# adaLN products of a two-layer mixer: split weights and VectorE sums replaced by unsplit float32 matmuls in four 128x32 tiles

## The chip, the cores and the metric

The kernel runs on one core of one Trainium2 chip. The metric is the device time of one execution in microseconds; the time before is the median of 3 runs. Profiles and traces show one execution each.

## What is computed

Two trunk layers work on 1024 latent tokens of 1024 channels and 256 context tokens. Cut to what matters here:

```python
sc, scc = silu(c), silu(c_ctx)
for l in range(2):
    shift, scale, gate = split(sc @ w_ada[l] + b_ada[l], 3)           # w_ada[l]: 1024 x 3072
    shift_c, scale_c, gate_c = split(scc @ w_ada[l] + b_ada[l], 3)
    hc = rms_norm(h_ctx, norm_g[l]) * (1 + scale_c) + shift_c
    hx = rms_norm(x, norm_g[l]) * (1 + scale) + shift
    px = hx @ w_in[l]                    # queries, keys, values, GLU pair, Fourier input, three gates
    y = concat(attention * silu(g_att), conv_branch * silu(g_conv), fourier * silu(g_four)) @ w_out[l]
    if l == 0:
        h_ctx = h_ctx + gate_c * y_ctx   # the same mixer on the context tokens
    x = x + gate * y
return rms_norm(x, final_g)
```

All is float32. The adaLN products are two vectors (latent and context stream) times a 1024 x 3072 matrix, once for each layer.

## The kernel before, in words

Large float32 products are made as three float32r matmuls: each operand is split into a high part (a rounded copy, mostly ScalarE, `split`, line 373) and the rest (a subtraction, line 374, on GpSimd or VectorE), and `mm3` (lines 160 to 162) adds high x high, high x low and low x high in PSUM.

The order on each engine is set by a scheduler from priorities and its own estimates of time. Code inside `later()` gets a low priority and fills gaps; `later(0)` lets a block take turns with what follows. Loads are issued by SP, in one queue, in the order that the scheduler chose. Every engine works its own list in order. TensorE's accumulators are eight PSUM banks; `mmx` hands out two `pt` banks and one `mm` bank in turn.

The program runs so. The first layer's scale and shift come as columns for two blocks of 128 channels at a time (`ada_cols`, four times, u = 0 to 3). They are needed by `norm_transpose`, which transposes normed tiles on TensorE, applies scale and shift on ScalarE (line 361) and splits the result on VectorE (lines 363, 365). Three groups of tokens (512, 512, 256) pass, and a first pair of tiles of `w_in`, the Fourier input, is multiplied at once (`Pair`, p0, p1, p2). Then, for each layer: the second layer's scale and shift (`ada1`, in layer 0 alone), the GLU input of the convolution (`glu(0)`, `glu(1)`), the Fourier branch, the convolution's 31 taps on VectorE (`conv_taps`, lines 499 and 506, inside `later()`), the Fourier gate (`gate_mul`, lines 464 and 465), the sums for the residual gate (`gate_sums`, inside `later()`), keys, queries with rotary, values, attention mixed with more projections (the convolution's norm `conv_norm`, line 525, among them), then `gate_reduce` and the output projection.

The adaLN products are made in three ways:

- First layer, scale and shift (`ada_cols`): weights of 512 rows x 256 columns are loaded (16 loads of 512 KB), split on ScalarE and VectorE or GpSimd, and multiplied by `s4`, four columns (high and low of both streams), line 254. The four rows that result are transposed back to columns (line 263) and combined on VectorE (lines 265 to 277).
- Second layer, scale and shift (`ada_sums`, `ada_cols1`): weights of 128 rows x 1024 columns are loaded, and VectorE sums weight times scalar over eight loads for each stream (lines 286 and 288); TensorE then sums over partitions with a one-column matmul for each block of 128 channels (line 297).
- Gates of both layers (`gate_sums`, `gate_reduce`): the same VectorE sums, the bias added on one partition (line 313), and a sum over the partitions on every partition with a full matmul of ones (line 321).

Of the kernel before, what the change touches and what calls it, by code (L numbers as in the profile page):

```python
# [41 lines left out]
def f32(t):  # L42
    return t.bitcast(F32)


class Bufs:
    """Buffers of 1024 words (latent tokens) and of 256 words (context tokens), handed out by hand."""
# [18 lines left out]
class Buf:  # L66
# [19 lines left out]
    def again(self, what, dtype, ctx=True):  # L86
        """the same memory under another name; without ctx the short part is put back"""
        if not ctx and self.ic is not None:
            self.owner.free[256].append(self.ic)
            self.ic = None  # L90
        parts = [None if i is None else self.owner.named(what, i, words, dtype)
                 for i, words in ((self.il, 1024), (self.ic, 256))]
        self.il = self.ic = None
        return Buf(self.owner, *parts)
# [8 lines left out]
class Four:  # L103
    """four short buffers in the place of a long one"""
# [14 lines left out]
def tile_backbone(ctx: ExitStack, tc: tile.TileContext, a, out):  # L119
# [26 lines left out]
    def mmx():  # L146
        """an accumulator where no attention is about"""
        turn[0] += 1
        return mm() if turn[0] % 3 == 0 else pt()

    @contextmanager
    def later(offset=100000):
        """instructions that only fill gaps, or without an offset take turns with those that follow"""
# [10 lines left out]
    def rstd_of(ss, n, scale):  # L164
        """(ss * scale + EPS) ** -0.5 for columns [128, n] by Newton's iteration. A step without its factor of
        -1/2 multiplies by -2, -8 and -512; a power of two in v and the sign of the first guess make up for it."""
# [17 lines left out]
    ident = const.tile([P, P], F32, name="ident")  # L184
    prm = const.tile([P, 96], F32, name="prm")
    s2 = const.tile([P, 2, NK], F32, name="s2")
    s4 = const.tile([P, NK, 4], F32R, name="s4")
# [7 lines left out]
    def load_params():  # L195
# [6 lines left out]
        sv = s2.rearrange("p s k -> p (s k)")  # L202
        th16 = sm.tile([P, 16], F32, name="rv")
        S.activation(th16, prm[:, 0:16], AF.Tanh, scale=0.5)
        V.scalar_tensor_tensor(out=sv, in0=th16, scalar=1.0, in1=prm[:, 0:16], op0=ALU.add, op1=ALU.mult)
        V.tensor_scalar(out=sv, in0=sv, scalar1=0.5, scalar2=None, op0=ALU.mult)
        # columns c high, c low, ctx high, ctx low
        s4v = s4.rearrange("p k (s x) -> p s k x", x=2)
        V.tensor_copy(out=s4v[:, :, :, 0], in_=s2)
        V.tensor_tensor(out=s4v[:, :, :, 1], in0=s2, in1=f32(s4v[:, :, :, 0]), op=ALU.subtract)  # L210
# [15 lines left out]
    # scale (1) and shift (0) of two blocks of channels: [section, stream, block]  # L226
# [8 lines left out]
    def ada_cols(u, his):  # L235
        """the first layer's scale and shift of both streams as columns, for the channels of blocks 2u, 2u + 1"""
        l = 0
        oo = av(), mm()
        los, chain = [], Chain()
        for sec in (1, 0):  # L240
            o = oo[sec][0:4, 0:256]
            for h in range(2):
                j = (1 - sec) * 2 + h
                raw, lo = chain.next("wada")
                los.append(lo)
                wh, wl = his[(4 * u + j) % len(his)].lat, los[j].lat
                c0 = sec * D + u * 256
                nc.sync.dma_start(out=raw.lat.rearrange("p (r c) -> p r c", r=4),
                                  in_=a["w_ada"][l, h * 512:(h + 1) * 512, c0:c0 + 256]
                                  .rearrange("(r p) c -> p r c", p=P))  # L250
                split(wh, wl, raw.lat, (G if (4 * u + j) % 3 == 2 else V))
                for r in range(4):
                    for i, w in enumerate((wh, wl)):
                        T.matmul(o, lhsT=s4[:, h * 4 + r, :], rhs=w[:, r * 256:(r + 1) * 256],
                                 start=(h == 0 and r == 0 and i == 0), stop=(h == 1 and r == 3 and i == 1))
        for z in los + [chain]:
            z.put()
        t = t512()[0:4]
        S.activation(t[:, 256:512], oo[1][0:4, 0:256], AF.Copy)
        V.tensor_copy(out=t[:, 0:256], in_=oo[0][0:4, 0:256])  # L260
        b = oo[1][:, 256:272]
        for j in range(4):
            T.transpose(out=b[:, 4 * j:4 * j + 4], in_=t[:, j * P:(j + 1) * P], identity=ident[0:4, 0:4])
        q = sm.tile([P, 16], F32, name="nwt")
        V.tensor_copy(out=q, in_=b)
        qv = q.rearrange("p (e k s x) -> p e s k x", e=2, k=2, s=2)
        c = adac[u]
        for sec in range(2):
            V.tensor_tensor(out=c[:, sec], in0=qv[:, sec, :, :, 0], in1=qv[:, sec, :, :, 1], op=ALU.add)
        b0 = cols["b_ada"] + 24 * l + 2 * u  # L270
        g0 = cols["norm_g"] + 8 * l + 2 * u
        for st in range(2):
            x = c[:, 1, st]
            V.scalar_tensor_tensor(out=x, in0=x, scalar=1.0, in1=prm[:, b0 + 8:b0 + 10], op0=ALU.add, op1=ALU.add)
            V.tensor_tensor(out=x, in0=x, in1=prm[:, g0:g0 + 2], op=ALU.mult)
            x = c[:, 0, st]
            V.tensor_tensor(out=x, in0=x, in1=prm[:, b0:b0 + 2], op=ALU.add)

    def ada_sums(l, sec, streams, acc, wbufs):
        """a section on the vector engine: partial sums over the partitions' rows"""  # L280
        for k in range(NK):
            w = wbufs[k % len(wbufs)]
            nc.sync.dma_start(out=w, in_=a["w_ada"][l, k * P:(k + 1) * P, sec * D:(sec + 1) * D])
            for st, z in zip(streams, acc):
                if k == 0:
                    V.tensor_scalar(out=z, in0=w, scalar1=s2[:, st, 0:1], scalar2=None, op0=ALU.mult)
                else:
                    V.scalar_tensor_tensor(out=z, in0=w, scalar=s2[:, st, k:k + 1], in1=z,
                                           op0=ALU.mult, op1=ALU.add)

    def ada_cols1(sec, acc):
        """the second layer's scale or shift as columns"""
        b = mmx()[:, 0:2 * NK]
        for st in range(2):
            for k in range(NK):
                j = st * NK + k
                T.matmul(b[:, j:j + 1], lhsT=acc[st][:, k * P:(k + 1) * P], rhs=onesm[:, 0:1], start=True, stop=True)
        b0 = cols["b_ada"] + 24 + 8 * sec
        g0 = cols["norm_g"] + 8
        for st in range(2):  # L300
            x = adac1[:, sec, st]
            V.scalar_tensor_tensor(out=x, in0=b[:, st * NK:(st + 1) * NK], scalar=256.0, in1=prm[:, b0:b0 + 8],
                                   op0=ALU.mult, op1=ALU.add)
            if sec:
                V.scalar_tensor_tensor(out=x, in0=x, scalar=1.0, in1=prm[:, g0:g0 + 8], op0=ALU.add, op1=ALU.mult)

    def gate_sums(l, streams, acc, wbufs):
        ada_sums(l, 2, streams, acc, wbufs)
# [593 lines left out]
    for z in his:  # L902
        z.put()
# [309 lines left out]
```

## Time and profile before

| what | value |
|---|---|
| runs (3) | 1306.56, 1308.06, 1308.09 us; median 1308.06 us |
| profiled execution | span 1303.3 us from the first instruction to the last; no other time of it is given; the runs lie 3.3 to 4.8 us above |
| TensorE (PE) | 1124.9 us busy, 86% of the span |
| VectorE (DVE) | 979.8 us, 75% |
| ScalarE (ACT) | 542.2 us, 42% |
| GpSimd (POOL) | 536.8 us, 41% |
| mean granted TensorE clock | 0.943 of full speed |
| loads and stores | 140.17 MB, 35.4% of the 16 DMA engines' span |

Times are in us from the start of the span unless marked ns. PE is TensorE, PEld its weight load, DVE VectorE, ACT ScalarE, POOL GpSimd, SP the queue that issues loads. L254 is line 254 of the kernel before. The ends of matmuls are modelled, and matmuls overlap: the distance between two starts tells more than the length of one. A float32 matmul shows as two records, a float32r matmul as one.

### The profile page before, as it was taken

The page shows a single profiled execution, that of the slowest core. Times are in us where ns is not written, and L with a number is a line of the kernel's source. Part 1 is how long each engine was busy: PE and PEld are TensorE (multiplying, and loading weights), DVE is VectorE, ACT ScalarE, POOL GpSimd, SP SyncE. Part 2 cuts the span into 40 slices and gives each one's busy share as a digit, 9 for nine tenths or more (in the row PEclk, how much of TensorE's full clock was granted, in tenths as well). Part 3 has the DMA queues.
Part 4 walks back from the last instruction along what each step waited for, and adds up shares of the span by engine and source line. Part 5 has one row for each costly group of instructions (what it writes and reads, how often), then busy time and mean ns, then how long its engine had stood idle before and what let it go on. Part 6 is the DMA issues. An engine that isn't in the chain of part 4 may idle for free.

```text
span 1303.3 us, 16751 instructions
## 1 busy us (share of the span) xinstructions
PE 1124.9 (86%) x5925; PEld 944.8 (72%) x5925; DVE 979.8 (75%) x1744; ACT 542.2 (42%) x1153; POOL 536.8 (41%) x353
## 2 busy tenths in 40 slices
PE   4877989697999999699879999988887999689977
PEld 2555877586778989578768777866766878478865
DVE  6899499999766566877766863999965466877755
ACT  6532222112265575255654442231215465465451
POOL 3425236445322231655434634264443221764322
PEclk9887989799998999899989999988998989899999
DMA  9634234132331322644425321532331223733313
GB/s 329 208 117 133 66 104 138 33 106 89 85 86 41 98 61 66 189 122 146 131 71 170 115 75 34 155 94 86 97 107 55 66 73 93 206 82 113 115 33 113
DMA packets 136156, 140.17 MB, mean 108 GB/s; under 512 B 6614, under 2 KB 114566, under 8 KB 136072
## 3 DMA queue, kind: packets, MB, share of 16 engines
q1 hardware_dynamic: 136072, 139.10, 35.4%
q8 instruction: 47, 0.77, 0.2%
q14 instruction: 37, 0.30, 0.1%
HBM read 107.35 MB, written 31.73 MB: 107 GB/s over the span
## 4 chain that ended last, share of the span: by engine, by line
PE 44%; DVE 35%; issue 7%; DMA 6%; ACT 3%; POOL 3%; SPq 0%; DVEq 0%; ACTq 0%; POOLq 0%
DVE cy L506 11%; PE mm L160 7%; PE mm L161 6%; PE mm L162 6%; PE avt L799 4%; PE pt L791 4%; PE pt L160 3%; PE pt L161 3%; PE pt L162 3%; PE score L761 2%; PE score L763 2%; DVE pl L795 2%; DVE score L773 2%; POOL q L708 2%; DMA wada<-w_ada 2%
## 5 line engine op out<-in xcount | busy, mean ns | idle before, releaser
L374 POOL TENSOR_TENSOR wl<-wr,wh 128x1024 fp32r<-128x1024 f32 x57 | 159.2, 2792 | 188.2 <-ACT wh L373 183.0
L506 DVE SCALAR_TENSOR_TENSOR cy<-cu,cw,cy 128x241 f32<-128x241 f32 (+27 forms) x168 | 211.3, 1290 | 0.4
L781 POOL TENSOR_SCALAR p<-p,st 128x640 f32<-128x640 f32 (+2 forms) x144 | 114.5, 807 | 235.7 <-DVE st L779 173.3
L160 PE MATMUL mm<-hxh,wh 128*128 128x512 f32 (+1 forms) x424 | 166.9, 394 | 20.3 <-DVE t L464 8.9
L160 PE MATMUL pt<-hxh,wh 128*128 128x512 f32 (+1 forms) x384 | 144.5, 381 | 36.4 <-DVE t L464 17.5
L161 PE MATMUL mm<-hxl,wh 128*128 128x512 f32 (+1 forms) x424 | 165.4, 390 | 2.3 <-DVE hxl L365 2.3
L162 PE MATMUL mm<-hxh,wl 128*128 128x512 f32 (+1 forms) x424 | 165.4, 390 | 0.7 <-POOL wl L374 0.7
L162 PE MATMUL pt<-hxh,wl 128*128 128x512 f32 (+1 forms) x384 | 143.8, 375 | 3.5 <-POOL wl L374 3.5
L161 PE MATMUL pt<-hxl,wh 128*128 128x512 f32 (+1 forms) x384 | 144.2, 376 | 1.3 <-DVE hxl L365 1.3
L795 DVE TENSOR_TENSOR pl<-pt,ph 128x512 fp32r<-128x512 f32 (+1 forms) x184 | 111.5, 615 | 40.2 <-ACT ph L794 39.3
L794 ACT ACTIVATE ph<-pt 128x512 fp32r<-128x512 f32 (+1 forms) x184 | 96.9, 540 | 93.0 <-PE pt L791 91.4
L373 ACT ACTIVATE wh<-wr 128x1024 fp32r<-128x1024 f32 x57 | 60.4, 1059 | 143.3 <-DMA wr<-w_in 77.1
L791 PE MATMUL pt<-ident,p 128*128 128x128 f32 x640 | 104.7, 284 | 17.2 <-DVE pl L795 13.3
L773 DVE CUSTOM_DVE_ANT_0 score<-score,mask,nsink 128x640 f32<-128x640 f32 (+2 forms) x128 | 103.7, 819 | 20.7 <-PE score L763 17.9
L775 ACT ACTIVATE p<-score,st 128x640 f32<-128x640 f32 (+2 forms) x144 | 105.2, 733 | 30.5 <-DVE st L773 24.0
L160 PEld LDWEIGHTS pt<-hxh,wh 128*128 128x128 f32 x384 | 77.5, 203 | 51.5 <-DVE t L464 18.2
L160 PEld LDWEIGHTS mm<-hxh,wh 128*128 128x128 f32 x424 | 83.6, 197 | 36.9 <-DVE t L464 9.5
L799 PE MATMUL avt<-ph,v 128*128 128x256 f32 x320 | 91.4, 309 | 11.3 <-DVE ot L807 9.6
L799 PE MATMUL avt<-pl,v 128*128 128x256 f32 x320 | 89.4, 302 | 11.7 <-DVE pl L795 11.4
L791 PEld LDWEIGHTS pt<-ident,p 128*128 128x128 f32 x640 | 78.5, 146 | 27.1 <-DVE pl L795 10.1
L161 PEld LDWEIGHTS mm<-hxl,wh 128*128 128x128 f32 x424 | 83.4, 197 | 16.6 <-DVE hxl L365 2.9
L162 PEld LDWEIGHTS mm<-hxh,wl 128*128 128x128 f32 x424 | 83.4, 197 | 16.0 <-POOL wl L374 1.1
(255 smaller groups left out, 2646.3 us busy)
## 6 DMA issues: line engine op xcount, KB each, us to landing
wada<-w_ada SPq DMA_DIRECT2D x48, 512.0 KB, 4.3
wr<-w_in SPq DMA_DIRECT2D x39, 512.0 KB, 4.0
qq<-qd SPq DMA_DIRECT2D x36, 256.0 KB, 4.2
x1d<-x SPq DMA_DIRECT2D x10, 512.0 KB, 3.3
od<-ot SPq DMA_DIRECT2D x18, 256.0 KB, 2.3
sg<-sgd SPq DMA_DIRECT2D x36, 128.0 KB, 2.8
wr<-od SPq DMA_DIRECT2D x18, 256.0 KB, 3.0
wr<-yd SPq DMA_DIRECT2D x18, 256.0 KB, 3.5
```

Of the source, the lines that this page charges most:

```text
L160: T.matmul(o, lhsT=lhs[0], rhs=rhs[0], start=start, stop=False)
L161: T.matmul(o, lhsT=lhs[0], rhs=rhs[1], start=False, stop=False)
L162: T.matmul(o, lhsT=lhs[1], rhs=rhs[0], start=False, stop=stop)
L374: E.tensor_tensor(out=lo, in0=raw, in1=f32(hi), op=ALU.subtract)
L506: V.scalar_tensor_tensor(out=z.cols(o0, o1), in0=u.cols(o0 + d, o1 + d), scalar=w(j), in1=z.cols(o0, o1), op0=ALU.mult, op1=ALU.add)
L773: V.tensor_tensor_reduce(out=sc[:, c0:768], in0=sc[:, c0:768], in1=mask[:, 640 - n:640], op0=ALU.add, op1=ALU.min, scale=1.0, scalar=ns, a ...
L775: S.activation(pp[:, i * n:(i + 1) * n], sc[:, c0:768], AF.Exp, scale=-1.0, bias=m1, accum_out=st[:, 6 + i:7 + i])
L781: G.tensor_scalar(out=pp[:, i * n:(i + 1) * n], in0=pp[:, i * n:(i + 1) * n], scalar1=st[:, 10 + i:11 + i], scalar2=1.0, op0=ALU.mult, op1 ...
L791: T.transpose(out=bt[:, (j * 2 + i) * P:(j * 2 + i + 1) * P], in_=pp[:, c0:c0 + P], identity=ident)
L794: S.activation(ph.cols(c0, c1), bt[:, :w * 256], AF.Copy)
L795: V.tensor_tensor(out=pl.cols(c0, c1), in0=bt[:, :w * 256], in1=f32(ph.cols(c0, c1)), op=ALU.subtract)
L799: T.matmul(o, lhsT=vv[kt][:, kv * P:(kv + 1) * P], rhs=z.cols(j * 256, (j + 1) * 256), start=(j == 0 and x == 0), stop=(j == nkt - 1 and x ...
```

## The change

All adaLN products become float32 matmuls without splits. `s2p` holds both streams' vectors in the first two of 32 columns, the rest zeros. A product (`ada_mm`) multiplies 128 rows of weights by 256 columns into 32 PSUM partitions; the products of four neighbouring row blocks go to the four column groups of the array (tiles of 128 rows x 32 columns), and two rounds of four cover the 1024 rows. So every group of 256 output columns is eight products, with four partial sums standing at partitions 0, 32, 64 and 96. `sel` adds them: a product with two columns for the columns of scale and shift (`ada_cols`, now for both layers), and with a broadcast `sel3`, which also picks the bias from partition 2, for the gate on all partitions (`gate_rows`). There are 64 products for each layer's scale and shift and 32 for each layer's gates, 192 in all, and 32 selection products in `ada_cols`.

`ada_sums`, `ada_cols1` and `gate_reduce` go. First-layer weights are loaded into eight buffers used in two halves, second-layer weights and gate weights into four; all 48 loads now have the form 512 rows x 256 columns. In attention the small copy buffer `otmp` is replaced by one of the four `t512` buffers. Comments are left out too. The diff, cut to this:

```diff
-    s2 = const.tile([P, 2, NK], F32, name="s2")
-    s4 = const.tile([P, NK, 4], F32R, name="s4")
+    s2p = const.tile([P, NK, 32], F32, name="s2p")
+    sel = const.tile([P, 2], F32, name="sel")
+    sel3 = const.tile([P, 2], F32, name="sel3")
...
+        G.memset(s2p, 0.0)
+        V.tensor_scalar(out=s2p.rearrange("p k x -> p x k")[:, 0:2, :], in0=th16.rearrange("p (s k) -> p s k", s=2),
+                        scalar1=0.5, scalar2=None, op0=ALU.mult)
+        V.tensor_tensor(out=sel, in0=ident[:, 0:2], in1=ident[:, 32:34], op=ALU.add)
+        for j in (64, 96):
+            V.tensor_tensor(out=sel, in0=sel, in1=ident[:, j:j + 2], op=ALU.add)
+        V.tensor_scalar(out=sel3, in0=sel, scalar1=ident[:, 2:3], scalar2=None, op0=ALU.add)
...
+    def ada_mm(l, sec, u, o, raws):
+        c0 = sec * D + u * 256
+        for h in range(2):
+            raw = raws[h]
+            nc.sync.dma_start(out=raw.rearrange("p (r c) -> p r c", r=4),
+                              in_=a["w_ada"][l, h * 512:(h + 1) * 512, c0:c0 + 256]
+                              .rearrange("(r p) c -> p r c", p=P))
+            for r in range(4):
+                T.matmul(o[32 * r:32 * r + 32, 0:256], lhsT=s2p[:, h * 4 + r, :], rhs=raw[:, r * 256:(r + 1) * 256],
+                         start=(h == 0), stop=(h == 1))
+
+    def ada_cols(l, u, raws, banks):
+        t = t512()
         for sec in (1, 0):
+            o = banks[sec]()
+            ada_mm(l, sec, u, o, raws[2 * sec:2 * sec + 2])
+            S.activation(t[:, sec * 256:(sec + 1) * 256], o[:, 0:256], AF.Copy)
+        o = banks[1]()[:, 0:8]
         for j in range(4):
+            T.matmul(o[:, 2 * j:2 * j + 2], lhsT=t[:, j * P:(j + 1) * P], rhs=sel, start=True, stop=True)
+        ov = o.rearrange("p (e k s) -> p e s k", e=2, k=2)
+        c = adac1[:, :, :, 2 * u:2 * u + 2] if l else adac[u]
...
+    def gate_sums(l, z, raws):
+        for u in range(4):
+            o = mmx()
+            ada_mm(l, 2, u, o, raws[u % 2 * 2:u % 2 * 2 + 2])
+            S.activation(z[:, u * 256:(u + 1) * 256], o[:, 0:256], AF.Copy)
         b0 = l * 3 * D + 2 * D
+        nc.sync.dma_start(out=z[2:3, :], in_=a["b_ada"][b0:b0 + D].rearrange("(o d) -> o d", o=1))
+
+    def gate_rows(z, streams, dst):
+        for st in range(streams):
+            sb = t512()[:, :P]
+            V.tensor_copy(out=sb, in_=sel3[:, st:st + 1].broadcast_to([P, P]))
             for h in range(2):
                 b = mm()
+                T.matmul(b, lhsT=sb, rhs=z[:, h * 512:(h + 1) * 512], start=True, stop=True)
+                S.activation(dst[st][:, h * 512:(h + 1) * 512], b, AF.Copy)
...
-            tmp = sm.tile([P, 256], F32, name="otmp", bufs=1)
+            tmp = t512()[:, :256]
...
-    his = [bufs.get("wadah", F32R) for _ in range(4)]
-    ada_cols(0, his)
+    ada_banks = (av, mm)
+    raws = [bufs.get("wada") for _ in range(8)]
+    half = lambda u: [z.lat for z in raws[u % 2 * 4:u % 2 * 4 + 4]]
+    ada_cols(0, 0, half(0), ada_banks)
...
-            z4 = [bufs.get("wada") for _ in range(5)]
-            z = [i.lat for i in z4]
+            z4 = [bufs.get("wada") for _ in range(4)]
             with later(0):
-                for sec in (1, 0):
-                    ada_sums(1, sec, [0, 1], z[:2], z[2:])
-                    ada_cols1(sec, z[:2])
+                for u in range(4):
+                    ada_cols(1, u, [z.lat for z in z4], (mmx, mmx))
...
-        wb_ = [bufs.get("wada") for _ in range(2)]
-        for st in gst:
-            gates[l, st] = bufs.get("gate")
-        ac_ = [gates[l, st].lat for st in gst]
+        gsum = bufs.get("gsum")
+        wb_ = [bufs.get("wada") for _ in range(4)]
         with later():
-            gate_sums(l, gst, ac_, [z.lat for z in wb_])
+            gate_sums(l, gsum.lat, [z.lat for z in wb_])
```

The scheduler also moves instructions. On SP, the loads at the program's start stand so before, where `x_` are latent input tiles, `wada_` first-layer adaLN weights and `wr` a tile of `w_in`:

```order
L248 DMA wada_444<-w_ada 128x4x256
L248 DMA wada_457<-w_ada 128x4x256
L248 DMA wada_470<-w_ada 128x4x256
L248 DMA wada_483<-w_ada 128x4x256
L717 DMA mask<-k_mask 128x640
L718 DMA nsink<-attn_sink 128x16
L721 DMA ar<-k_alt 128x2
L399 DMA wr<-w_in 128x8x128
L222 DMA x_552<-x 128x1024
```

and so with the change, at the place where the third set of weights begins:

```order
L244 DMA wada_146<-w_ada 128x4x256
L225 DMA x_414<-x 128x1024
L225 DMA x_416<-x 128x1024
L225 DMA x_418<-x 128x1024
L225 DMA x_420<-x 128x1024
L225 DMA x_459<-ctx 128x1024
L225 DMA x_461<-ctx 128x1024
L244 DMA wada_143<-w_ada 128x4x256
L684 DMA mask<-k_mask 128x640
```

Before, all sixteen loads of weights stand ahead of the second and third groups' inputs; with the change the six inputs stand ahead of the last eight loads of weights.

On TensorE, between the first tile pair and `glu(0)`, the rows before are these (L482 the convolution's parameters, L571 the Fourier matrices, the rest GLU):

```order
L482 MATMUL pt<-ident,t_868 128x62 x2
L571 MATMUL pt<-wf_890,t_892 128x256 x2
L162 MATMUL mm<-hxh_297,wl 128x512
L160 MATMUL mm<-hxh_301,wh 128x512
L161 MATMUL mm<-hxl_303,wh 128x512
L162 MATMUL mm<-hxh_301,wl 128x512
```

and with the change (L449 and L538 are the first two of them, L248 the second layer's products, L260 their selection, L575 a Fourier term):

```order
L449 MATMUL pt<-ident,t_732 128x62 x2
L538 MATMUL pt<-wf_754,t_756 128x256 x4
L248 MATMUL mm<-wada_806,s2p 32x256 x4
L248 MATMUL mm<-wada_807,s2p 32x256 x4
L248 MATMUL pt<-wada_804,s2p 32x256 x4
L248 MATMUL pt<-wada_805,s2p 32x256 x4
L575 MATMUL avt<-fu_463,wf_754 128x1
L575 MATMUL avt<-fu_465,wf_754 128x1
L260 MATMUL pt<-sel,t_808 128x2 x4
L575 MATMUL avt<-fu_463,wf_754 128x1
L575 MATMUL avt<-fu_465,wf_754 128x1
L248 MATMUL mm<-wada_806,s2p 32x256 x4
```

Twenty-four more products follow ahead of GLU's first matmul, on the same four buffers 804 to 807; the last twelve stand among GLU's.

On VectorE, ahead of the second GLU part's result (`cu`), taps (`cy`) and gate sums take turns before:

```order
L506 SCALAR_TENSOR_TENSOR cy_1443<-cu_1033,cw,cy_1443 128x1017
L288 SCALAR_TENSOR_TENSOR gate_1947<-wada_1946,s_75,gate_1947 128x1024
L288 SCALAR_TENSOR_TENSOR gate_1948<-wada_1946,s_75,gate_1948 128x1024
L506 SCALAR_TENSOR_TENSOR cy_1444<-cu_1034,cw,cy_1444 128x251
L506 SCALAR_TENSOR_TENSOR cy_1443<-cu_1033,cw,cy_1443 128x1016
L965 SCALAR_TENSOR_TENSOR cu_1507<-p_1509,pt 128x512
```

and with the change taps alone stand there (L473 is the tap, L934 the GLU result):

```order
L473 SCALAR_TENSOR_TENSOR cy_1362<-cu_952,cw,cy_1362 128x1011
L473 SCALAR_TENSOR_TENSOR cy_1363<-cu_953,cw,cy_1363 128x245
L473 SCALAR_TENSOR_TENSOR cy_1362<-cu_952,cw,cy_1362 128x1010
L934 SCALAR_TENSOR_TENSOR cu_1426<-p_1428,mm 128x512
L473 SCALAR_TENSOR_TENSOR cy_1363<-cu_953,cw,cy_1363 128x244
```

Between the first two GLU results and the last Fourier gate product of the first layer, 72 taps and 16 gate products and sums stand on VectorE before, and 91 taps with the change; from there to the convolution's norm 46 taps before, 27 now. In the second layer the two counts are 36 and 20 before, 40 and 16 now.

## Rows read from the trace of the kernel before

**Rows 1.** The page: busy time by engine, chain by engine, the taps' group.
```profile
PE 1124.9 (86%) x5925; PEld 944.8 (72%) x5925; DVE 979.8 (75%) x1744; ACT 542.2 (42%) x1153; POOL 536.8 (41%) x353
...
PE 44%; DVE 35%; issue 7%; DMA 6%; ACT 3%; POOL 3%; SPq 0%; DVEq 0%; ACTq 0%; POOLq 0%
...
L506 DVE SCALAR_TENSOR_TENSOR cy<-cu,cw,cy 128x241 f32<-128x241 f32 (+27 forms) x168 | 211.3, 1290 | 0.4
```

**Rows 2.** By stretch: length, busy PE, PEld, DVE, ACT, POOL, clock, DMA share, GB/s.
```profile
46.00:105.10 59.10, 46.26 (x238) 36.47 (x235) 54.19 (x100) 22.50 (x38) 21.36 (x15) 0.88 0.37 114
105.10:152.70 47.60, 37.98 (x191) 32.37 (x190) 28.19 (x35) 10.74 (x17) 18.88 (x9) 0.86 0.37 111
152.70:271.90 119.20, 98.19 (x493) 83.83 (x492) 118.30 (x118) 26.02 (x38) 51.12 (x17) 0.90 0.28 90
271.90:383.90 112.00, 98.25 (x521) 82.86 (x520) 90.20 (x144) 33.66 (x82) 50.87 (x26) 0.97 0.32 91
...
807.60:900.90 93.30, 82.48 (x382) 68.86 (x381) 90.05 (x71) 22.67 (x31) 39.63 (x14) 0.93 0.36 108
900.90:999.00 98.10, 82.43 (x370) 66.64 (x369) 76.60 (x94) 26.54 (x54) 43.35 (x19) 0.95 0.32 94
```

**Rows 3.** The same view of the saturated start, 5 to 45 us.
```profile
5.00:45.00 40.00, 26.68 (x158) 16.45 (x159) 33.98 (x61) 26.30 (x34) 16.39 (x6) 0.96 1.07 352
```

**Rows 4.** Instructions on the weights: count, ns min/median/max, first and last start.
```profile
L288 DVE SCALAR_TENSOR_TENSOR wada<-wada,s,wada x28: 1269/1273/3367, 68.4 to 130.0; 128x1024 f32<-128x1024 f32 x28
L288 DVE SCALAR_TENSOR_TENSOR gate<-wada,s,gate x21: 1265/1273/3383, 199.2 to 860.3; 128x1024 f32<-128x1024 f32 x21
...
L373 ACT ACTIVATE wadah<-wada x16: 1041/1057/1061, 10.1 to 42.2; 128x1024 fp32r<-128x1024 f32 x16
L374 DVE TENSOR_TENSOR wada<-wada,wadah x11: 1204/1224/1226, 11.2 to 49.0; 128x1024 fp32r<-128x1024 f32 x11
```

**Rows 5.** Timeline of PE: start, length, instruction; xN are N records together.
```profile
26.04 0.28 PE L254 MATMUL mm<-wada,s 128*4 128x256 f32 x1
26.15 0.28 PE L254 MATMUL mm<-wadah,s 128*4 128x256 f32 x1
...
81.56 0.60 PE L356 MATMUL score<-ident,x 128*128 128x128 f32 x4
...
95.82 4.00 PE L297 MATMUL mm<-onesm,wada 128*128 128x1 f32 x32 [0.72 <-DVE wada L288]
...
787.23 1.02 PE L571 MATMUL pt<-wf,t 128*128 128x256 f32 x4
```

**Rows 6.** Timeline: the last first-layer columns, two neighbouring float32r matmuls.
```profile
58.18 0.23 DVE L275 TENSOR_TENSOR ada<-ada,prm 128x2 f32<-128x2 f32 x2
...
607.05 0.39 PE L162 MATMUL mm<-wo,wl 128*128 128x512 f32 x1
607.27 0.39 PE L160 MATMUL mm<-wo,wh 128*128 128x512 f32 x1
```

**Rows 7.** Loads: count, KB each, median us from issue to landing.
```profile
wada<-w_ada SPq DMA_DIRECT2D x48, 512.0 KB, 4.3
wr<-w_in SPq DMA_DIRECT2D x39, 512.0 KB, 4.0
```

**Rows 8.** By stretch, one line alone: L506, L288, L288; busy DVE, clock, DMA.
```profile
152.70:271.90 119.20, 69.02 (x68) 0.90 0.28 90
...
152.70:271.90 119.20, 27.15 (x14) 0.90 0.28 90
...
807.60:900.90 93.30, 8.92 (x7) 0.93 0.36 108
```

**Rows 9.** Waits of PE and ACT, 271.9 to 383.9, then ACT, 383.9 to 807.6.
```profile
PE pt L160 <- ACT q L471: 9.8, 2, 8.5
...
ACT q L471 <- DVE cy L509: 8.0, 1, 8.0
...
ACT otmp L805 <- PE avt L799: 28.8, 16, 6.1
```

More of the change, by code (lines that the diff above doesn't have):

```diff
@@ L201, in load_params @@
         V.tensor_copy(out=prm, in_=pb[:, :96])
-        sv = s2.rearrange("p s k -> p (s k)")
         th16 = sm.tile([P, 16], F32, name="rv")
         S.activation(th16, prm[:, 0:16], AF.Tanh, scale=0.5)
[L205 to L210, printed above, removed]
+        V.scalar_tensor_tensor(out=th16, in0=th16, scalar=1.0, in1=prm[:, 0:16], op0=ALU.add, op1=ALU.mult)
+        G.memset(s2p, 0.0)
[5 more added lines that the diff above has]
+        V.tensor_scalar(out=sel3, in0=sel, scalar1=ident[:, 2:3], scalar2=None, op0=ALU.add)
         V.memset(onesm, 1.0 / 256.0)
@@ L233, in tile_backbone @@
     gates = {}
[L235 to L239, printed above, removed]
-        for sec in (1, 0):
[L241 to L261, printed above, removed]
-        for j in range(4):
[L263 to L269, printed above, removed]
@@ L273, in ada_cols @@
             x = c[:, 1, st]
-            V.scalar_tensor_tensor(out=x, in0=x, scalar=1.0, in1=prm[:, b0 + 8:b0 + 10], op0=ALU.add, op1=ALU.add)
+            V.scalar_tensor_tensor(out=x, in0=ov[:, 1, st], scalar=1.0, in1=prm[:, b0 + 8:b0 + 10],
+                                   op0=ALU.add, op1=ALU.add)
             V.tensor_tensor(out=x, in0=x, in1=prm[:, g0:g0 + 2], op=ALU.mult)
[L276 to L305, printed above, removed]
@@ L307, in gate_sums @@
-    def gate_sums(l, streams, acc, wbufs):
-        ada_sums(l, 2, streams, acc, wbufs)
-        b0 = l * 3 * D + 2 * D
-        nc.sync.dma_start(out=wbufs[0][0:1, :], in_=a["b_ada"][b0:b0 + D].rearrange("(o d) -> o d", o=1))
-        for z in acc:
-            V.tensor_tensor(out=z[0:1, :], in0=z[0:1, :], in1=wbufs[0][0:1, :], op=ALU.add)
-    def gate_reduce(acc):
-        for z in acc:
+            V.tensor_tensor(out=c[:, 0, st], in0=ov[:, 0, st], in1=prm[:, b0:b0 + 2], op=ALU.add)
+    def gate_sums(l, z, raws):
[3 more added lines that the diff above has]
+            S.activation(z[:, u * 256:(u + 1) * 256], o[:, 0:256], AF.Copy)
+        b0 = l * 3 * D + 2 * D
+        nc.sync.dma_start(out=z[2:3, :], in_=a["b_ada"][b0:b0 + D].rearrange("(o d) -> o d", o=1))
@@ L318, in gate_reduce @@
+    def gate_rows(z, streams, dst):
+        for st in range(streams):
+            sb = t512()[:, :P]
+            V.tensor_copy(out=sb, in_=sel3[:, st:st + 1].broadcast_to([P, P]))
             for h in range(2):
-                zz = z[:, h * 512:(h + 1) * 512]
                 b = mm()
-                T.matmul(b, lhsT=onesm, rhs=zz, start=True, stop=True)
-                S.activation(zz, b, AF.Copy, scale=256.0)
+                T.matmul(b, lhsT=sb, rhs=z[:, h * 512:(h + 1) * 512], start=True, stop=True)
+                S.activation(dst[st][:, h * 512:(h + 1) * 512], b, AF.Copy)
@@ L893, in tile_backbone @@
         if u < 3:
-            ada_cols(u + 1, his)
+            ada_cols(0, u + 1, half(u + 1), ada_banks)
         else:
@@ L901, in tile_backbone @@
         p0.step(two)
-    for z in his:
+    for z in raws:
         z.put()
@@ L977, in ada1 @@
                 return
-            z4 = [bufs.get("wada") for _ in range(5)]
-            z = [i.lat for i in z4]
+            z4 = [bufs.get("wada") for _ in range(4)]
             with later(0):
-                for sec in (1, 0):
-                    ada_sums(1, sec, [0, 1], z[:2], z[2:])
-                    ada_cols1(sec, z[:2])
-            for i in z4:
-                i.put()
+                for u in range(4):
+                    ada_cols(1, u, [z.lat for z in z4], (mmx, mmx))
+            for z in z4:
+                z.put()
         ada1()
@@ L1075, in tile_backbone @@
             f()
-        gate_reduce(ac_)
+        for st in gst:
+            gates[l, st] = bufs.get("gate")
+        gate_rows(gsum.lat, len(gst), [gates[l, st].lat for st in gst])
+        gsum.put()
         wo = load_wout(l)
```

## The prediction

> **What bounds the kernel now.** The page comes first [rows 1]: TensorE is busy for 86% of the span and VectorE for 75%, but the chain that ended last is 44% TensorE and 35% VectorE, so two engines bound it in turn. The table by stretch shows where [rows 2]; its ends are the end of the first input tile pair (105.1), the first layer's GLU chunk that releases the convolution taps (152.7), the last Fourier gate product (271.9), the start of the convolution norm (383.9), and the same three places of the second layer (807.6, 900.9, 999). VectorE is busy for 54.2 of 59.1 us before 105.1, for 118.3 of 119.2 us from 152.7 and for 90.1 of 93.3 us from 807.6; elsewhere TensorE is the busier one. From 5 to 45 us a third limit stands: the DMA share is 1.07 at 352 GB/s [rows 3]. The adaLN work sits in these very stretches [rows 4]: splits on VectorE, 28 sums of 1.27 us and more for the second layer, 21 for the gates. So the change relieves VectorE where it binds; the price is time on TensorE. That price decides.
>
> **The price of a product.** The trace has no float32 product on 32 columns. The nearest row is the full-width float32 matmul of 256 columns [rows 5]: two records each, starting 0.215 us apart ((1.02 - 0.38) / 3), so 0.43 us per product. That is the upper end, tiles one after another. If all four tiles worked at once it would be a quarter, 0.11 us, the lower end. I take 0.215, for a reason in the order of work: a product's two records need the same 32 columns, so the second must follow the first, but the next product's first record needs other columns and can run beside it; two at once in program order gives half. Nothing in the trace tells that tiles overlap at all. The Trainium skill ("TensorE: Matmul & The Clock Gate", Part 3) gives 2.38 for three column tiles side by side; on 0.43 us that would be an estimate of 0.18 us and a total of 1277 us, and no run here shows it.
>
> On TensorE 192 products come, 41 us at 0.215 and 83 us at 0.43, with 32 selection products (two records of 0.12 us like L297's, (4.00 - 0.28) / 31 [rows 5], 8 us). 128 L254 matmuls, 0.115 us apart at full clock, and 64 L297 records go [rows 5]: 15 and 8 us. So TensorE gains 26 to 68 us of work while VectorE loses about 90 (28 and 21 sums with their first products, 11 splits). The sum must go by stretch.
>
> **Step 1, to the last first-layer scale.** The new SP order puts six x loads ahead of the last eight weight loads. Ahead of and with the last one stand 28 loads of 0.524 MB and 0.7 MB of small ones, 15.4 MB; at 352 GB/s from 1.2 us on they land at 45 us. Now the last weights are landed long before, but wait for splits (16 of 1.06 us on ScalarE, 11 of 1.22 us on VectorE [rows 4]), and the last columns are written at 58.4 [rows 6]. After: 45, plus eight products (1.7), four selections (1.0) and some 1.3 us for a copy and six column operations, which come in pairs of 0.23 us [rows 6]: 49. Gain 9.4.
>
> **Step 2, to the end of the first tile pair.** Behind it on TensorE stand 56 transposes at 0.11 us ((0.60 - 0.28) / 3), 74 matmuls of 512 columns at 0.23 us, 48 of 256 at 0.12 us [rows 5, 6] and eight second-layer products: 30.6 us, and 3 for handovers, ending at 83. VectorE keeps some 30 of its 54 us there (15 sums, two first products and two splits leave [rows 4]), so TensorE sets it by little. Before: 105.1. Gain now 22.
>
> **Step 3, to the taps.** Here the change gives back. Second-layer products stand in a row ahead of GLU's first matmul, and TensorE runs in order, so GLU waits behind products that wait for loads. Four buffers are filled in two pairs; a pair is reloaded once its products are done. A load issues in 0.45 us and lands in 4.3 [rows 7], its products take 1.7, so a pair turns in 6.5 us and two pairs give a group each 3.25 us: five groups and the first lead are 18 us. Behind them: 25.3 us of GLU (96 matmuls of 512 and 24 of 256 columns), 3.8 of Fourier (32), 2.6 of twelve products, 1.9 of eight selections. With 3.5 us for the half clock (this stretch ran at 0.86 [rows 2]) the taps start at 138, against 152.7: gain 14.7. Whether the rows of weights are 4 KB or 1 KB I cost at nothing, since loads of 512-byte rows land in 4.0 us [rows 7]; SP's later loads wait behind the reloads, inside the same 18 us.
>
> **Step 4, taps to the last gate product.** Out go 14 gate sums (27.2 us [rows 8]), two first products and two bias sums, which I take at 1 us each, below the sums' 1.27 [rows 4]: 31 us. But the scheduler moves taps up: 91 instead of 72 stand there, and 68 took 69.0 us [rows 8], so 19 more are 19.3 us. VectorE still binds. Gain 11.7.
>
> **Step 5, to the convolution norm.** 46 taps become 27, VectorE falls from 90 to about 71 of 112 us and TensorE (98.3 busy [rows 2]) binds. It gets 32 gate products, 6.9 us. Of its 9.8 us of waits on ScalarE, which itself waited 8.0 us for VectorE's taps [rows 9], I take back 5. Loss 2.
>
> **Step 6, second layer.** Seven sums (8.9 us [rows 8]), one first product and one bias sum (1 us each) go from the VectorE-bound 93.3 us; four taps move up (4.1): gain 6.8. The next 98.1 us are TensorE's (82.4 busy [rows 2]): 6.9 more, 2.6 back from waits. Net gain 2.5.
>
> **The rest.** The gate rows are the same six full-width matmuls, with three small copies. The attention's copy now takes one of four shared buffers; ScalarE's waits there are for TensorE's results (28.8 us [rows 9]), which hides it; without that cover 72 copies could cost or save some 3 us. The load of s2p, sel and their zeros lies before the first weights at 10 us. I cost all three at nothing.
>
> **The sum.** 14.7 + 11.7 - 2 + 2.5 = 26.9 off the span of 1303.3 gives 1276.4. The runs' median is 4.8 above that span, so the forecast is **1281 us**. With 0.11 us the same steps give 17.7 + 11.7 + 1.6 + 6 = 37, with 0.43 they give 4.7 + 11.7 - 8.8 - 4.4 = 3.2: 1271 and 1305.
>
> **The rivals.**
> - *Four tiles at once*: 0.11 us, **1271**. For it: four products in a row write four different column groups. Against it: each product's second record needs its own first one done.
> - *One after another*: 0.43 us, **1305**, no change. For it: the only float32 rows here are serial. Shown by starts 0.215 us apart throughout.
> - *Slower: TensorE drained at each change of tile width*, on top of serial products. A record lasts 0.38 us while the next starts after 0.215, so 0.16 us of overlap is lost at each change; 24 groups have 48 changes, 7.8 us: **1313**. It decides once a product with its share of drains costs over 0.46 us. Against it: L254 already uses 4 columns between full-width matmuls and loses nothing visible [rows 5]. The Trainium skill ("TensorEngine Tiling (Array Packing)", Tiling Modes, Key Properties) says that a change of tiling mode, not of tile, drains TensorE; by that rule the result is this rival's, and no row of the trace has such a change to agree or not.
> - *Taps that cost more*: they now meet GpSimd's work at other times. The page's mean is 1.29 us with waits, the stretch's 1.01 [rows 1, 8]; 91 taps at 1.29 take back 25 us: **1306**.
>
> **How the numbers follow.** A measurement here tells about 0.2% (2.6 us) from no change. Chances: forecast 0.45, four at once 0.17, one after another 0.16, drains 0.14, dearer taps 0.08. The forecast's own range is 1268 to 1294, since steps 2 and 3 are uncertain by some 6 us each. Over all cases 1260 to 1315 leaves out 2 in 10. Faster: most of the first two, half of the third: 0.68. Same 0.11. Slower, nearly all from the drains and a part of the serial case: 0.21.
>
> **What would show it.** Right: L248 records about 0.11 us apart in pairs, or a group of eight within 1.9 us; the taps starting near 138; VectorE still full until the last gate product, TensorE fuller behind it; no L286 or L288. Step 1 is wrong if the last weights land well off 45 us; step 3 if GLU's first matmul does not wait for w_ada loads; step 4 if VectorE idles there. The forecast falls if starts lie 0.215 us apart, or if gaps of 0.2 us stand at each change between 32 and 128 columns.

## The result and the profile after

The change makes the kernel slower: 1364.58 us against 1307.85 us (medians of 4 runs each), a ratio of 1.044 with a 95% interval of 1.0419 to 1.0461. The forecast was 1281 us, its range 1260 to 1315. The profiled execution has a span of 1359.1 us, 55.8 more than before.

The page of the changed kernel, to set beside [rows 1]: busy time by engine, and the chain by engine.

```profile
PE 1152.2 (85%) x6165; PEld 950.1 (70%) x6165; DVE 874.0 (64%) x1681; ACT 533.3 (39%) x1157; POOL 494.0 (36%) x349
...
PE 33%; DVE 13%; DMA 6%; ACT 4%; issue 3%; POOL 2%; SPq 0%; DVEq 0%; ACTq 0%; POOLq 0%
```

VectorE did lose 106 us of work, and TensorE gained only 27. The price was low and the relief came, yet the span grew. The table by stretch of the changed kernel shows where (columns as in [rows 2]). Its ends are the end of the first tile pair (81.7), the first product in a row ahead of GLU (88.2), GLU's first matmul (106.8), the taps (143), the last Fourier gate product (254.3), the convolution norm (380), and the same places of layer 2 (828, 921, 1019.9).

```profile
46.00:81.70 35.70, 34.96 (x240) 28.35 (x238) 22.44 (x47) 16.73 (x29) 7.15 (x7) 1.00 0.31 96
81.70:88.20 6.50, 3.10 (x11) 1.95 (x10) 3.80 (x6) 4.71 (x10) 6.50 (x6) 0.90 0.53 155
88.20:106.80 18.60, 13.73 (x113) 6.42 (x112) 2.70 (x19) 2.65 (x7) 3.33 (x2) 0.59 0.89 281
106.80:143.00 36.20, 36.08 (x202) 29.70 (x199) 4.52 (x16) 6.61 (x10) 7.16 (x3) 0.94 0.17 56
143.00:254.30 111.30, 86.95 (x469) 72.47 (x468) 110.90 (x117) 25.64 (x38) 51.70 (x16) 0.92 0.29 93
254.30:380.00 125.70, 117.32 (x641) 97.98 (x640) 81.01 (x161) 46.58 (x120) 43.78 (x35) 0.99 0.31 87
380.00:828.00 448.00, 382.49 (x2016) 323.12 (x2014) 270.38 (x626) 206.03 (x468) 167.52 (x141) 0.93 0.32 96
828.00:921.00 93.00, 74.47 (x367) 60.43 (x366) 85.19 (x65) 22.27 (x31) 38.82 (x14) 0.90 0.27 86
921.00:1019.90 98.90, 95.85 (x463) 77.94 (x464) 66.88 (x90) 28.84 (x58) 38.40 (x19) 0.95 0.39 114
1019.90:1359.00 339.10, 279.71 (x1499) 236.93 (x1497) 206.34 (x468) 153.65 (x354) 116.04 (x95) 0.93 0.29 87
```

Two stretches of the kernel before have no row ahead of the prediction, since I expected nothing there. They run from each layer's convolution norm to the next layer, or to the end, and hold most of the attention.

```profile
383.90:807.60 423.70, 383.74 (x2086) 328.64 (x2086) 282.15 (x662) 217.10 (x503) 175.49 (x150) 0.95 0.34 102
999.00:1303.30 304.30, 267.85 (x1497) 228.00 (x1496) 205.00 (x465) 154.32 (x354) 118.57 (x95) 0.96 0.33 97
```

Up to the last Fourier gate product the change is ahead: 254.3 against 271.9, so 17.6 us. Then the way to the convolution norm is 13.7 us longer (125.7 against 112.0), the first attention stretch 24.3 and the second 34.8. In these two TensorE has 65.5 and 59.4 us without work, where it had 40.0 and 36.4 (length less busy): 48.5 of the 59.1 us lost are idle TensorE, and the granted clock falls from 0.95 and 0.96 to 0.93. Neither stretch holds an adaLN product; only six small gate-row matmuls and one new buffer are there.

ScalarE's timeline shows the buffer at work. L772 copies an attention result into it; L420 is the first operation of a projection's gate and takes a buffer of the same four. The lines of the changed kernel between are left out:

```profile
409.42 0.58 ACT L420 ACTIVATE t<-mm 128x512 f32<-128x512 f32 x1
...
418.49 0.60 ACT L420 ACTIVATE t<-mm 128x512 f32<-128x512 f32 x1 [4.26 <-PE mm L162]
...
423.87 0.37 ACT L420 ACTIVATE t<-mm 128x256 f32<-128x256 f32 x1
424.26 0.38 ACT L772 ACTIVATE t<-avt 64x256 f32<-64x256 f32 x1
430.56 0.38 ACT L772 ACTIVATE t<-avt 64x256 f32<-64x256 f32 x1 [5.92 <-PE avt L766]
...
434.16 0.38 ACT L772 ACTIVATE t<-avt 64x256 f32<-64x256 f32 x1
...
437.49 0.38 ACT L772 ACTIVATE t<-avt 64x256 f32<-64x256 f32 x1 [0.61 <-PE avt L766]
437.89 0.60 ACT L420 ACTIVATE t<-mm 128x512 f32<-128x512 f32 x1
```

Three, four, three, four: one projection, one attention block, and so on. In the same view of the kernel before, the two kinds (L453, L805) mix, mostly one by one:

```profile
417.69 0.59 ACT L453 ACTIVATE t<-mm 128x512 f32<-128x512 f32 x1
...
421.69 0.38 ACT L805 ACTIVATE otmp<-avt 64x256 f32<-64x256 f32 x1
...
426.14 0.60 ACT L453 ACTIVATE t<-mm 128x512 f32<-128x512 f32 x1 [4.08 <-PE mm L162]
...
427.98 0.38 ACT L805 ACTIVATE otmp<-avt 64x256 f32<-64x256 f32 x1 [0.25 <-PE avt L799]
...
432.87 0.37 ACT L453 ACTIVATE t<-mm 128x256 f32<-128x256 f32 x1
433.26 0.38 ACT L805 ACTIVATE otmp<-avt 64x256 f32<-64x256 f32 x1
```

The program text says why. It writes an attention block, then a projection that is to fill its gaps, six times over in the first layer and four times in the second. A block asks for four buffers, a projection for three (two in layer 2), and the four buffers go round in the order of asking. With a shared set the projection's first temporary waits for the block's copies and the next block's copies wait for the projection's temporaries, so neither fills the other's gaps. This was theory A; theory B was that the attention suffers from something else in the change.

### The profile page after: what moved, and what is told of

Its sections match the earlier page's. It is cut to its first block, busy times and chain, and to the rows that moved or that the text cites. A ratio compares the mean times of both kernels' runs of the same rounds, so it can differ in the third digit from the quotient of the medians.

```text
span 1359.1 us, 17095 instructions
## 1 busy us (share of the span) xinstructions
PE 1152.2 (85%) x6165; PEld 950.1 (70%) x6165; DVE 874.0 (64%) x1681; ACT 533.3 (39%) x1157; POOL 494.0 (36%) x349
## 4 chain that ended last, share of the span: by engine, by line
PE 33%; DVE 13%; DMA 6%; ACT 4%; issue 3%; POOL 2%; SPq 0%; DVEq 0%; ACTq 0%; POOLq 0%
PE mm L160 5%; PE mm L161 5%; PE mm L162 5%; DVE cy L473 4%; PE pt L160 3%; PE pt L161 3%; PE pt L162 3%; PE avt L766 3%; PE pt L758 2%; PE score L728 2%; POOL wl L341 1%; DMA wr<-od 1%; DMA qq<-qd 1%; DVE score L740 1%; ACT p L742 1%
## 5 line engine op out<-in xcount | busy, mean ns | idle before, releaser
L341 POOL TENSOR_TENSOR wl<-wr,wh 128x1024 fp32r<-128x1024 f32 x57 | 156.0, 2737 | 231.1 <-ACT wh L340 200.5
L748 POOL TENSOR_SCALAR p<-p,st 128x640 f32<-128x640 f32 (+2 forms) x144 | 111.3, 786 | 281.9 <-DVE st L746 144.3
L473 DVE SCALAR_TENSOR_TENSOR cy<-cu,cw,cy 128x1013 f32<-128x1013 f32 (+24 forms) x168 | 210.1, 1290 | 1.0
L160 PE MATMUL mm<-hxh,wh 128*128 128x512 f32 (+1 forms) x408 | 158.1, 387 | 34.4 <-DVE t L431 19.1
L160 PE MATMUL pt<-hxh,wh 128*128 128x512 f32 (+1 forms) x400 | 151.9, 384 | 7.4 <-DVE t L431 7.4
L162 PE MATMUL mm<-hxh,wl 128*128 128x512 f32 (+1 forms) x408 | 154.6, 379 | 0.9 <-POOL wl L341 0.9
L161 PE MATMUL mm<-hxl,wh 128*128 128x512 f32 (+1 forms) x408 | 155.3, 381 | 0.0
L161 PE MATMUL pt<-hxl,wh 128*128 128x512 f32 (+1 forms) x400 | 151.6, 380 | 0.0
L162 PE MATMUL pt<-hxh,wl 128*128 128x512 f32 (+1 forms) x400 | 150.9, 378 | 0.1
L160 PEld LDWEIGHTS mm<-hxh,wh 128*128 128x128 f32 x408 | 82.4, 202 | 52.2 <-DVE t L431 20.3
L766 PE MATMUL avt<-ph,v 128*128 128x256 f32 x320 | 89.2, 306 | 14.8 <-DVE ot L774 7.5
L728 PE MATMUL score<-kh,q 128*128 128x384 f32 (+1 forms) x128 | 53.5, 418 | 47.1 <-DVE q L702 32.4
L160 PEld LDWEIGHTS pt<-hxh,wh 128*128 128x128 f32 x400 | 76.8, 194 | 23.0 <-DVE t L431 8.3
L162 PEld LDWEIGHTS mm<-hxh,wl 128*128 128x128 f32 x408 | 81.7, 200 | 13.8 <-POOL wl L341 1.3
```

The lines of the kernel that those rows point to most:

```text
L160: T.matmul(o, lhsT=lhs[0], rhs=rhs[0], start=start, stop=False)
L161: T.matmul(o, lhsT=lhs[0], rhs=rhs[1], start=False, stop=False)
L162: T.matmul(o, lhsT=lhs[1], rhs=rhs[0], start=False, stop=stop)
L341: E.tensor_tensor(out=lo, in0=raw, in1=f32(hi), op=ALU.subtract)
L473: V.scalar_tensor_tensor(out=z.cols(o0, o1), in0=u.cols(o0 + d, o1 + d), scalar=w(j), in1=z.cols(o0, o1), op0=ALU.mult, op1=ALU.add)
L748: G.tensor_scalar(out=pp[:, i * n:(i + 1) * n], in0=pp[:, i * n:(i + 1) * n], scalar1=st[:, 10 + i:11 + i], scalar2=1.0, op0=ALU.mult, op1 ...
```

## The experiments

Times are medians. Each ratio is to runs of the kernel before taken beside the run (medians of 1304 to 1306 us).

**The buffer alone, in the kernel before** (e1_before_shared).

```diff
-            tmp = sm.tile([P, 256], F32, name="otmp", bufs=1)
+            tmp = t512()[:, :256]
```

> The kernel before with one edit of the change alone: the attention's copy (line 805) takes one of the four shared t512 buffers instead of its own otmp. Theory A (the shared buffers tie the attention to the projections that fill its gaps, so both attention stretches lose some 25 and 35 us): 1345 to 1370 us, with no change before the convolution norm at 384. Theory B (the attention loses through something else: the order that follows from moved taps, the gate rows, the clock): 1305 to 1311, as before.

Measured: 1372.88 us, ratio 1.0511 (1.0476 to 1.0546), just above the range of theory A and far from theory B. This one line costs 68.6 us, more than the whole change loses. Its two attention stretches:

```profile
400.40:848.90 448.50, 390.02 (x2034) 328.40 (x2033) 267.06 (x625) 206.33 (x468) 170.82 (x141) 0.93 0.31 95
1041.10:1376.00 334.90, 280.87 (x1498) 237.74 (x1496) 204.44 (x466) 153.78 (x354) 116.57 (x95) 0.92 0.30 88
```

They are 24.8 and 30.6 us longer than before, close to the changed kernel's 24.3 and 34.8. A part was not expected: the convolution norm starts at 400.4 instead of 383.9. Counted in the trace, 102 attention matmuls stand between the last Fourier gate product and the norm where the kernel before has 50. The changed kernel has 102 there too, so its 13.7 us between 254.3 and 380 are of the same kind. Most of this is order and not lost time: by 400.4 TensorE has started as many records here as it had by 395.6 in the kernel before, some 5 us behind by that count, and by the end of the first attention stretch (848.9) it is some 41 us behind. So nearly all of the loss lies behind the norm.

**The change with its own buffer** (e2_changed_own), with the control for the layout that makes room (e3_changed_narrow, without the last pair of lines).

```diff
-    s2p = const.tile([P, NK, 32], F32, name="s2p")
+    s2p = const.tile([P, 46], F32, name="s2p")
...
-            ... lhsT=s2p[:, h * 4 + r, :]
+            ... lhsT=s2p[:, 2 * (h * 4 + r):2 * (h * 4 + r) + 32]
...
-            tmp = t512()[:, :256]
+            tmp = sm.tile([P, 256], F32, name="otmp", bufs=1)
```

> The change with otmp put back as a buffer of the attention's own; to make room, the 32 columns of each product's vectors now overlap in a tile of 46 columns, so that rows 2 to 31 of a tile hold other products, which the selection multiplies by zero. Theory A: the attention's loss of 59 us goes and what the early stages gained stays, 1290 to 1305 us. Theory B: 1355 to 1368, as the change.

> Control for the run before it: the change with the overlapping 46 columns alone, the attention's copy still in the shared buffers. Both theories: as the change, 1358 to 1368 us; off it by more, and the layout of the vectors would have a part in the difference.

Measured: 1293.95 us, ratio 0.9921 (0.9893 to 0.9949), and 1362.45 us, ratio 1.0454 (1.0424 to 1.0484), for the control. The two differ by the buffer alone, so the buffer is the whole loss: without that edit the adaLN products make the kernel 0.8% faster. The attention stretches of the first:

```profile
368.40:789.30 420.90, 376.81 (x2060) 320.39 (x2059) 281.29 (x657) 215.85 (x498) 173.66 (x148) 0.95 0.34 104
...
980.40:1288.50 308.10, 271.05 (x1498) 230.83 (x1496) 205.34 (x467) 154.57 (x354) 118.91 (x95) 0.95 0.32 96
```

**The tie cut at its other end** (e5_partner_leaves). The copy stays in the shared buffers; the projections between the blocks get their own.

```diff
-            th = t512()[:, :c1 - c0]
+            th = zb.cols(c0, c1)
...
+            zb = bufs.get("th", ctx=wc)
```

> The mirror of the run with its own otmp: the attention's copy stays in the four shared t512 buffers (46 columns of vectors as in the control), and the projections that are written between the attention blocks (attention gate and convolution gate) get a buffer of their own each instead. Theory A, made sharper (the four buffers go round in the order in which the program text asks for them, so an attention block's four copies and the three temporaries of the projection written behind it must alternate, and neither can run ahead to fill the other's gaps): the tie is cut at its other end, 1285 to 1305 us. Rival (the copy into the shared buffer is itself dearer, or any copy without its own buffer waits): 1355 to 1368, as the change.

Measured: 1300.16 us, ratio 0.9962 (0.9943 to 0.9981), some 6 us above the own-buffer version. Of the control's loss 62 us are gone though the copy still goes into a shared buffer, so the copy is not dear in itself; the partner in the round is what costs. The order on ScalarE in the first layer's attention agrees: blocks of four copies and three temporaries stand in the changed kernel, in e1, in the control and in the run that comes next, and the two kinds mix in the kernel before, in the own-buffer version and in this one. A larger shared set, with more than four buffers, was not tried.

**The projection written first** (e10_projection_first), as in the control but with `f()` ahead of `att(...)` in the loop.

> The change as it was (attention's copy in the four shared buffers, 46 columns of vectors), with each projection written ahead of its attention block instead of behind it. Theory A (the buffers go round in the order of the text, so copies and temporaries still alternate, whichever comes first): the loss stays for the most part, 1335 to 1370 us. If only the place of the text mattered, because the projection is then there to fill: 1290 to 1310.

Measured: 1341.65 us, ratio 1.0273 (1.0226 to 1.0319). Some 21 of the control's 1362 us come back, the rest of the loss stays: the order of the text sets how large it is, the shared round that there is one.

**The price of a product** (e4_changed_serial): with the own buffer, all eight products of a group in one column group.

```diff
-                T.matmul(o[32 * r:32 * r + 32, 0:256], ..., start=(h == 0), stop=(h == 1))
+                T.matmul(o[0:32, 0:256], ..., start=(h == 0 and r == 0), stop=(h == 1 and r == 3))
```

> On top of the change with its own otmp: all eight products of a group go into the first column group, so that none stands beside another, and copies and selections take 32 partitions. If four tiles side by side run at once (0.43 us for four products, as starts 7 ns apart in the changed kernel's trace say), each product now costs 0.43 us: 192 products 62 us more TensorE work, of which some 25 lie in stretches where TensorE binds: 15 to 35 us above the run with its own otmp. If the records only look parallel and four products cost the same either way, the time is that run's within 5 us.

Measured: 1336.79 us, 42.8 above the own-buffer version, which is more than the 35 expected. Of the 46.9 us between the two spans 33.2 arise ahead of the first layer's convolution norm (401.6 against 368.4). Two timelines show the records, 16 for eight products. The changed kernel, first at half clock, then with a wait for a load, and last at full clock:

```profile
88.23 1.94 PE L248 MATMUL mm<-wada,s2p 128*32 128x256 f32 x16
...
95.81 1.08 PE L248 MATMUL mm<-wada,s2p 128*32 128x256 f32 x8 [2.04 <-DMA wada<-w_ada]
...
121.38 0.39 PE L162 MATMUL mm<-hxh,wl 128*128 128x512 f32 x1
121.70 1.07 PE L248 MATMUL pt<-wada,s2p 128*32 128x256 f32 x16
122.70 0.39 PE L160 MATMUL mm<-mh,eo 128*128 128x256 f32 x1
```

and the run with one column group:

```profile
106.04 3.64 PE L248 MATMUL mm<-wada,s2p 128*32 128x256 f32 x16
```

One group: (3.64 - 0.38) / 15 = 0.217 us per record. Four groups: four records start together (7 ns apart), so 16 are four rounds of (1.07 - 0.38) / 3 = 0.23 us. A product costs two records of a quarter round, 0.115 us, against 0.43 in a row; that is 3.8 times as fast.

**The gates put back to VectorE sums** (e6_gate_sums_back), all else as in the own-buffer version.

> The own-otmp version with the residual gates alone put back to VectorE sums (21 sums and their first products, bias on one partition, ones matmul); first and second layer's scale and shift stay float32 products. If the gate sums' 31 us on VectorE were in the way of the gate products as step 4 said, with the taps that move up again in part: 8 to 16 us above the own-otmp version's 1294. If VectorE's relief there is worth nothing because other work ends last: within 4 us of it.

Measured: 1316.49 us, 22.5 above it, more than the 16 expected. The spans differ by 26.0, as the own-buffer version's profiled execution lies 3.2 us below its median: 10.6 up to the last Fourier gate product (265.7 against 255.1), 6.7 from there to layer 2's convolution norm, 8.7 behind it. The first is what step 4 called for. The last is not explained by any sum, since none is left there; it stays open.

**More buffers for layer 2's products** (e7_eight_buffers).

```diff
-            z4 = [bufs.get("wada") for _ in range(4)]
+            z4 = [bufs.get("wada") for _ in range(8)]
...
-                    ada_cols(1, u, [z.lat for z in z4], (mmx, mmx))
+                    ada_cols(1, u, [z.lat for z in z4[u % 2 * 4:u % 2 * 4 + 4]], (mmx, mmx))
```

> The own-otmp version with eight buffers in two halves, in place of four, for the second layer's products. If reloads of four buffers hold TensorE ahead of GLU, as step 3 said: some 5 to 8 us less than 1294 (TensorE was idle for 6.5 of the 22.8 us from 84.0 to 106.8 in the changed kernel). If the DMA engines are what binds there (share 0.80, 250 GB/s in that stretch): within 3 us of 1294.

Measured: 1285.74 us, ratio 0.9855 (0.982 to 0.989), 8.2 below four buffers. The stretch of the row of products:

```profile
88.20:106.80 18.60, 15.85 (x146) 10.09 (x144) 2.97 (x20) 4.16 (x9) 3.31 (x2) 0.96 0.71 227
```

Against the change's row for the same times: 33 more matmuls, and a clock of 0.96 in place of 0.59. The first long tap starts at 137.4 instead of 144.2, and all of that reaches the end.

**The products elsewhere.** Spread behind the gate, key and query projections (e8_products_spread); behind the first GLU projection, with eight buffers (e9_products_behind_glu); between the two GLU projections, Fourier behind both, eight buffers (e11_second_glu_first).

> The own-otmp version with the second layer's products taken away from ahead of GLU and written one group each behind the two Fourier gate projections, the keys and the first queries. If their place, not their number, costs (the 18.7 us from 88.2 to 106.9 in which TensorE worked on nothing else): taps start 13 to 18 us sooner and nearly all of it carries to the end, since VectorE binds to the last Fourier gate product: 1278 to 1284 us. If TensorE binds where they go, or their loads hold it there: 1288 to 1296.

> The version with eight buffers, with the second layer's products moved from ahead of the GLU projections to behind the first of them. There TensorE had to wait 11.8 us for GpSimd's split of the Fourier matrices in the run with spread products, so the products' time is covered. If so, taps start some 25 us sooner than in the eight-buffer version (137.4) and about half of it is left at the last Fourier gate product: 1270 to 1279 us. If the head start is lost again as in the run with spread products (the Fourier branch waits, VectorE has no taps left to do): 1284 to 1310.

> The version with eight buffers, with both GLU projections ahead of the Fourier branch and the second layer's products between the two. In the run with the products behind the first GLU, VectorE was busy for 113.6 of the 130 us from 110 to 240 and waited 11.0 us for the second GLU's result, which stood behind products and Fourier. If that wait was what ate the head start: VectorE stays full, the last Fourier gate product falls near 232 instead of 246: 1270 to 1279 us. If TensorE's own work and the Fourier branch's chain decide there, whatever VectorE does: 1282 to 1300.

Measured: 1308.7, 1286.35 and 1292.27 us. All three start the taps some 25 to 30 us sooner than the version that they change (first tap at 112.9, 112.6 and 110.2; with the products ahead of GLU 144.2 with four buffers and 137.4 with eight), and none gains by it; e8 falls outside both expectations. It has four buffers: its last Fourier gate product ends at 248.6, against 255.1 in the own-buffer version, so 6.5 us are left of the head start. In e9 and e11 it ends at 246.8 and 249.1, against 245.8 with eight buffers. In e8, from 113 to 249, TensorE waits for GpSimd's split of the Fourier matrices, and a group of products waits for VectorE's half of a Fourier gate:

```profile
PE score L161 <- POOL dft L341: 11.8, 1, 11.8
...
PE mm L248 <- DVE t L431: 10.0, 1, 10.0
```

Behind it e8 loses more than it gained: from the last gate product to the norm it takes 134.9 us (248.6 to 383.5) where the own-buffer version takes 113.3. There the moved products wait for their weights, and a projection waits for ScalarE's copy of their results:

```profile
PE pt L248 <- DMA wada<-w_ada: 5.9, 1, 5.9
PE pt L160 <- ACT t L257: 5.5, 1, 5.5
```

So the second expectation had the reason right, TensorE and the loads, and the size too small.

In e9, from 110 to 247, VectorE waits for the second GLU part, which stands behind products and Fourier:

```profile
DVE cu L934 <- PE mm L162: 11.0, 1, 11.0
```

In e11 that wait is gone, and the end comes no sooner. 112 taps stand ahead of the last gate product where the eight-buffer version has 86, and still VectorE is idle for 19.9 of the 138.9 us between its first tap and there, 8.7 of them in one wait for ScalarE's part of a Fourier gate. So VectorE alone does not end that stretch. Whether Fourier's chain or TensorE's order does it there, these runs do not separate.

## Why the prediction was wrong, point by point

The step that failed is **the rest**, where the copy into the shared buffers stood at nothing: "which hides it; without that cover 72 copies could cost or save some 3 us". I priced the copies, and looked for what hides them. What the edit changed was who else takes those buffers, and in what order. The cost is not in any copy (0.38 us before and after) but in the gaps between them: 59.1 us in the two attention stretches, and 68.6 us for the edit alone.

The other steps, by the changed kernel and the own-buffer version:

- **The price of a product.** Taken at 0.215 us; it is 0.115, my lower end, so the rival *four tiles at once* had the price right, though not the time. My argument that a product's second record must follow its first agrees with the rows (0.217 us apart in one group), but the other three groups' records start with it. The Trainium skill's 2.38 ("TensorE: Matmul & The Clock Gate", Part 3) is for three tiles. With four, this trace shows 3.8, so the 0.18 us estimated from that figure was too high as well.
- **Drains at a change of tile width.** L248 starts 0.32 us behind L162, where L162's own kind starts 0.23 apart, and L160 0.31 behind the last round, where rounds are 0.23 apart: some 0.09 us at each change. By the rule in the Trainium skill ("TensorEngine Tiling (Array Packing)", Tiling Modes, Key Properties) a drain was due. The rows show no more than these 0.09 us, and 48 changes at that price, as an estimate, would be 4.3 us, against 7.8 in the prediction.
- **Steps 1 and 2.** The last first-layer weights whose landing the trace has land at 45.4 (forecast 45), the last columns are written at 52.6 (49), and the first tile pair ends at 81.7 (83).
- **Step 3.** The taps start at 143 (138): gain 9.7 instead of 14.7. The row of products took 18.6 us (18) and the rest 36.2 (37). Not in my sum were the 6.5 us from 81.7 to 88.2, where TensorE's transposes wait 1.1 us for ScalarE and its Fourier matrices 2.3 us for VectorE. The reloads hold TensorE as step 3 said, and cost more than waits: the clock is at 0.59, and eight buffers give 8.2 us back.
- **Step 4.** VectorE stays full (110.90 of 111.30), gain 7.9 instead of 11.7. The taps that moved up were the term mis-sized: in the own-buffer version 88 stand there, at 93.96 us, where [rows 8] with 19 more make 88.3. The rival *dearer taps* had the direction right (1.07 us each against 1.01), not the size.

```profile
143.30:255.10 111.80, 93.96 (x88) 0.89 0.28 92
```

- **Step 5.** In the own-buffer version the stretch is 113 us (255.1 to 368.4), a loss of 1 where I had 2. The changed kernel's 13.7 belong to the buffer, mostly as attention work moved ahead of the norm.
- **Step 6.** No gain in the first part (93.0 against 93.3, forecast 6.8) and 0.8 lost in the second. VectorE is no longer full there (85.19 of 93.00).

With the own buffer the span is 14.8 us shorter than before, where I had 26.9, and 37 at the low price. So the sum was too high even without the failed step: at that price step 3 by 8, step 4 by 4, step 5 by 3 and step 6 by 6, with 1 more in the attention stretches. The serial run shows that the price matters at least as much as the prediction said: 42.8 us, where its two ends lay 34 apart.

## What to carry to other kernels

A buffer that is merged into a shared, rotating set should be costed by its new neighbours: list who else takes from the set while it is in use, in the order of the program text, and ask which two streams must now alternate. If two streams are meant to fill each other's gaps, give them separate sets; here 1 KB per partition was worth 5%. Starting an engine's work sooner gained nothing in three tries here: the head start went into waits for other engines, or was lost again behind the stretch. So move work only after checking, on every engine, the end of the stretch and the place that the work moves to.

## What was not expected of the hardware

Float32 products on four column groups of 32 ran 3.8 times as fast as on one (0.23 us for four records against 0.217 for one), while each product needs two records on the same columns. Where TensorE worked in short bursts between loads, the granted clock was 0.59 over 18.6 us; with the loads ahead, in the same stretch, 0.96: eight products then take 1.07 us and not the 1.94 they take at 1.2 GHz.
